# A hybrid attention layer on one core: where the stick-breaking output norm is written, and which engine adds the two halves of an attention output

## Chip, core and metric

The kernel runs on one core of one Trainium2 chip. The metric is device time in microseconds, from the first to the last instruction and what lies around them; lower is better. The five engines each work through their own queue in order: PE (TensorE, matmuls; PEld is its weight load), ACT (ScalarE), DVE (VectorE), POOL (GpSimd) and SP (SyncE, which here issues the DMA transfers).

## What is computed

One layer of a transformer step for 1088 tokens: 1024 of a prompt and 64 of a sample with 128 cached positions. Eight heads use stick-breaking attention, eight use forgetting attention (a causal softmax with a bias), each of 64 channels. Each group of eight heads has an RMS norm of its own over its 512 channels, and then comes one output projection. Cut to what the change touches:

```python
o_sb = sb_prompt(q_sb, k_sb, v_sb)            # 8 heads, each a = exp(...) then a @ v
o_fx = fox_prompt(q_fx, k_fx, v_fx, f_cum)    # 8 heads, softmax(...) @ v
o = concatenate([rmsnorm(o_sb, g_sb_out), rmsnorm(o_fx, g_fox_out)], axis=-1)
x = x + (1.0 + ada[2]) * (o @ w_o)
# rmsnorm(x, g) = x * rsqrt(mean(x * x) + 1e-6) * g ; a SwiGLU FFN follows
```

## The kernel before

Products of fp32 numbers are made of two rounded halves each (hi and lo), so one product is three matmuls (L429, L430, L431, 24 for a block of 128 channels with its 1024 inputs). Channels lie on the 128 partitions, tokens along the free axis, in three chunks CH of 384, 384 and 320 tokens.

The 16 heads go in eight pairs (loop L992 to L1006): pairs 0 to 3 are stick-breaking, 4 to 7 forgetting. For each pair the code writes, in this order, the load of the next pair's weights, attention(pr), project_pair(pr + 1), values, setup of the next pair's head 0, low_finish(), setup of head 1, and low_job(pr + 1). A scheduler puts each engine's instructions in an order of its own, so products of the next pair's projection run among the attention of this one; but tiles of one tag share a fixed number of buffers, and PSUM has eight banks: "acc" 1 (projection products), "z" 3 (scores), "t" 2 (transposes), "u" 1, "av" 1.

attention(pr) (L669) goes through two heads, each with nine query tiles in the order 6, 7, 0, 1, 4, 5, 2, 3, 8, wide ones in two parts, so 13 parts to a head. Of a forgetting head, each part is scored in ps_z (L693, L696, mask L700), its maximum taken by DVE (L721; negated in nm, L727 or L730), its exp made by ACT into a_t (L733, tag "zs", six buffers), normalised by POOL (L739), transposed by PE into pt_a (L748), rounded by ACT (L443) with the rest by DVE (L754), and multiplied by the values into ps_av (L757). In a stick-breaking head sigmoids and a scan kp (L712) stand in place of the exp. av_out (L655) adds the two halves of ps_av into ot: in pairs 0 to 3 by an ACT copy (L662) and a POOL sum (L663), in pairs 4 to 7 by one DVE reduce (L665). L667 stores ot to oT_d in HBM. A hook of attention is a function that is called behind a step; below pair 7 a step is a head.

The norm of the stick-breaking outputs. low_job(5) writes o_stats: the outputs of pairs 0 to 3 are loaded back (L141), added, squared (L829) and summed into sqacc (L831, L834; tag "low", one buffer), beside attention(5). low_finish then writes token_cols (L198) once per chunk: matmuls L204 of 128 tokens by a column of ones into a "u" bank, a scale and epsilon (L212, L215), and rstd_cols (Sqrt on ACT, L191, and five DVE operations, L192 to L196) into cols_sb[c]. low_job(6) then writes sb_norm(0) and sb_norm(2), so ahead of attention(6): spread (L223) broadcasts the columns into a bank bc_o ("u" for chunk 0, "acc" for chunk 2), sum_o (L836, four times) loads an output's two parts o and o_lo (o_lo of tag "zs", as a_t) and adds them on POOL (L840), and DVE scales them (L897). sb_norm(1) and the splits for the output projection are in sb_ready, ahead of attention(7).

Of the kernel before, what the change touches and what calls it, by code (L numbers as in the profile page):

```python
# [8 lines left out]
F32 = mybir.dt.float32  # L9
# [3 lines left out]
ALU = mybir.AluOpType  # L13
# [3 lines left out]
P = 128  # L17
# [4 lines left out]
T = NP + NS  # L22
# [6 lines left out]
CH = ((0, 384), (384, 384), (768, 320))  # L29
# [32 lines left out]
HK = (1, 2)  # L62
# [3 lines left out]
SBT = ('u', 'acc', 'acc')  # L66
SBE = (0, 2)
# [22 lines left out]
def f32(ap):  # L90
    return ap.bitcast(F32)
# [3 lines left out]
def tile_hybrid_trunk(  # L95
# [11 lines left out]
    act, dve, pool, pe, sync = nc.scalar, nc.vector, nc.gpsimd, nc.tensor, nc.sync  # L107
# [13 lines left out]
    for kind, base in (("sb", -1), ("fox", 0)):  # L121
# [4 lines left out]
            out=mf, in_=mf, pattern=[[-1, P]], compare_op=ALU.is_ge,  # L126
# [59 lines left out]
    def bank(tag, name):  # L186
        return ps.tile([P, 512], F32, tag=tag, bufs=bank_bufs[tag], name=name)
# [10 lines left out]
    def token_cols(sqs, toks, count, col, tag="u"):  # L198

        pc = bank(tag, "pc")  # L200
        n = len(toks)
        for j, (a, w) in enumerate(toks):
            for i, sq in enumerate(sqs):
                pe.matmul(  # L204
                    out=pc[:w, j:j + 1], lhsT=sq[:, a:a + w], rhs=ones[:, 0:1],
                    start=(i == 0), stop=(i == len(sqs) - 1))
        v, tmp = col[:, 0, 0:n], col[:, 1, 0:n]
        last = toks[-1][1]
        full = n if last == P else n - 1
        if full < n:  # L210
            dve.memset(v[:, full:n], 1.0)
            dve.tensor_scalar(  # L212
                out=v[:last, full:n], in0=pc[:last, full:n], scalar1=1.0 / count, scalar2=EPS,
                op0=ALU.mult, op1=ALU.add)
        dve.tensor_scalar(  # L215
            out=v[:, 0:full], in0=pc[:, 0:full], scalar1=1.0 / count, scalar2=EPS, op0=ALU.mult, op1=ALU.add)
        rstd_cols(v, tmp)

    def spread(out_bank, col, toks):

        o = 0
        for j, (_, w) in enumerate(toks):
            pe.matmul(  # L223
                out=out_bank[:, o:o + w], lhsT=col[:w, 0, j:j + 1].to_broadcast([w, P]),
                rhs=ident[:w, :w], start=True, stop=True)
            o += w

    def chunk_toks(c, base=0):
        c0, n = CH[c]
        return tuple((base + a, min(P, n - a)) for a in range(0, n, P))  # L230
# [8 lines left out]
    ap1 = attA.enter_context(tc.tile_pool(name="attA1", bufs=1))  # L239
# [29 lines left out]
    def t_low(name, dt=F32):  # L269
        return ap1.tile([P, T], dt, tag="low", name=name)  # L270
# [17 lines left out]
    def load_x(c):  # L288
# [15 lines left out]
    pv = bank("u", "pv")  # L304
# [8 lines left out]
        out=cs4[:, :, 2:4], in0=csil.rearrange("p s k -> p k s"), in1=f32(cs4[:, :, 0:2]), op=ALU.subtract)  # L313
# [341 lines left out]
    def av_out(ps_av, pr, hb, qt):  # L655

        c0, n, t0 = (0, P, qt * P) if qt < 8 else (P - NS, NS, NP)
        ot = ap2.tile([P, 2, P], F32, tag="ot", bufs=OB, name="ot")
        pv = ps_av.rearrange("p (i q) -> p i q", i=2)[:, :, c0:c0 + n]
        piece = ot[:, 0, :n]  # L660
        if pr < 4:
            act.copy(out=ot[:, :, :n], in_=pv)  # L662
            pool.tensor_tensor(out=piece, in0=piece, in1=ot[:, 1, :n], op=ALU.add)  # L663
        else:
            dve.tensor_reduce(  # L665
                out=piece, in_=pv.rearrange("p i q -> p q i"), axis=mybir.AxisListType.X, op=ALU.add)
        sync.dma_start(out=oT_d[pr, hb].rearrange("i d t -> (i d) t")[:, t0:t0 + n], in_=piece)  # L667

    def attention(pr, heads, hooks):  # L669
# [148 lines left out]
    def o_stats(c, acc):  # L818

        t0, n = CH[c]  # L820
        for i in range(0, 4, 2):
            both = [
                t_.rearrange("p a b -> p (a b)")[:, 0:2 * n].rearrange("p (k t) -> p k t", k=2)
                for t_ in (t_lowraw(), f32(ap1.tile([P, 4, 256], F32R, tag="ada_l", name="sq_l")))]
            for k in range(2):
                load_o([t_[:, k] for t_ in both], i + k, t0, n)
            sq = both[0]
            pool.tensor_tensor(out=sq, in0=sq, in1=both[1], op=ALU.add)
            act.activation(sq, sq, AF.Square)  # L829
            if i == 0:  # L830
                pool.tensor_tensor(out=acc, in0=sq[:, 0], in1=sq[:, 1], op=ALU.add)  # L831
            else:
                for k in range(2):
                    pool.tensor_tensor(out=acc, in0=acc, in1=sq[:, k], op=ALU.add)  # L834
# [42 lines left out]
    vv0 = values(0, raws[2])  # L877
    heads = [setup(0, hb, raws[0], raws[1], vv0) for hb in range(2)]
    x1 = [[None] * 3 for _ in range(KT)]
    cols_sb = [ap1.tile([P, 2, 3], F32, name=f"cols_sb{c}") for c in range(3)]  # L880

    sb_o = [None] * 3

    def sb_norm(c, tag):

        t0, n = CH[c]
        bc = bank(tag, "bc_o")
        spread(bc, cols_sb[c], chunk_toks(c))
        if c < 2:
            o = [t_[:, a:a + n] for t_ in (t_low("o32"), t_lowraw().rearrange("p a b -> p (a b)")) for a in (0, n)]  # L890
        else:
            t_ = ap1.tile([P, 4, 256], F32, tag="ada_l", name="o32").rearrange("p a b -> p (a b)")
            o = [t_[:, a:a + n] for a in (0, n, 2 * n)] + [ap1.tile([P, n], F32, tag="small", name="o32_3")]
        for k in range(4):
            sum_o(o[k], k, t0, n, pool)
        for k in range(4):
            dve.scalar_tensor_tensor(  # L897
                out=o[k], in0=o[k], scalar=go[:, k:k + 1], in1=bc[:, :n], op0=ALU.mult, op1=ALU.mult)
        sb_o[c] = o
# [7 lines left out]
    def low_job(pr):  # L907

        for job in JOBS[pr]:
            ada_job(job)  # L910
        if pr == 6:
            for c in SBE:
                sb_norm(c, SBT[c])
        if pr != 5:
            return lambda: None
        acc = t_low("sqacc")
        for c, (t0, n) in enumerate(CH):
            o_stats(c, acc[:, t0:t0 + n])

        def finish():  # L920
            for c, (t0, n) in enumerate(CH):
                token_cols([acc[:, t0:t0 + n]], chunk_toks(c), 512, cols_sb[c])
        return finish


    fxh = [[None] * 3 for _ in range(4)]
# [62 lines left out]
        sb_split(1)  # L989

    low_finish = low_job(0)
    for pr in range(8):  # L992
        if pr < 7:
            wqk = load_qk(pr + 1)
        if pr == 7:
            sb_ready()
        attention(pr, heads, {HK[0]: fox_first, HK[1]: fox_second} if pr == 7 else {})
        if pr < 7:
            raws = project_pair(pr + 1, *wqk)
            vv1 = values(pr + 1, raws[2])  # L1000
            heads = [setup(pr + 1, 0, raws[0], raws[1], vv1)]
            low_finish()
            if pr == FG:
                forget_gates()
            heads.append(setup(pr + 1, 1, raws[0], raws[1], vv1))
            low_finish = low_job(pr + 1)  # L1006
# [627 lines left out]
```

## Time and profile before

| | |
|---|---|
| device time, median of 3 runs | 1635.71 us (1634.99 to 1638.09) |
| the profiled execution's own time | 1636.31 us |
| its span, first to last instruction | 1634.5 us |
| busy in the span | PE 94%, DVE 65%, ACT 49%, POOL 47% |
| mean granted clock of PE, of full speed | 0.973 |

Times in the rows are microseconds from the span's start. A row of a timeline gives start, length, engine, line and operation, output and inputs by the program's names, shapes and count, and in brackets the engine's idle time before it with what ended that. A row of stretches gives the stretch and its length, then the busy time of each engine with its count of instructions, PE's granted clock, the share of the DMA engines and GB/s. ACT, DVE and POOL busy times are those of their own instructions; matmul ends are modelled, so neighbouring matmuls overlap in the rows.

### The profile page before, as it was taken

The page shows a single profiled execution, that of the slowest core. Times are in us where ns is not written, and L with a number is a line of the kernel's source. Part 1 is how long each engine was busy: PE and PEld are TensorE (multiplying, and loading weights), DVE is VectorE, ACT ScalarE, POOL GpSimd, SP SyncE. Part 2 cuts the span into 40 slices and gives each one's busy share as a digit, 9 for nine tenths or more (in the row PEclk, how much of TensorE's full clock was granted, in tenths as well). Part 3 has the DMA queues.
Part 4 walks back from the last instruction along what each step waited for, and adds up shares of the span by engine and source line. Part 5 has one row for each costly group of instructions (what it writes and reads, how often), then busy time and mean ns, then how long its engine had stood idle before and what let it go on. Part 6 is the DMA issues. An engine that isn't in the chain of part 4 may idle for free.

```text
span 1634.5 us, 26657 instructions
## 1 busy us (share of the span) xinstructions
PE 1541.7 (94%) x9558; PEld 1445.6 (88%) x9558; DVE 1061.0 (65%) x2061; ACT 804.2 (49%) x1684; POOL 768.4 (47%) x681
## 2 busy tenths in 40 slices
PE   8899998999899986998999999999999999999998
PEld 4698887978788875888999999999999999999997
DVE  5656666578448464667785676657656666666665
ACT  5466656678255553554454454534433333333335
POOL 1557767675668785494343444442222222222222
PEclk9999999999899996999999999999999999999998
DMA  9533332421535463273325554442221222222211
GB/s 305 177 110 93 109 100 85 113 79 29 129 96 141 118 164 90 62 229 95 90 65 155 149 150 146 150 130 77 84 80 51 78 66 64 78 78 78 65 39 78
DMA packets 223204, 174.68 MB, mean 107 GB/s; under 512 B 15488, under 2 KB 213536, under 8 KB 223072
## 3 DMA queue, kind: packets, MB, share of 16 engines
q1 hardware_dynamic: 223072, 172.97, 36.7%
q8 instruction: 76, 1.25, 0.3%
q14 instruction: 56, 0.46, 0.1%
HBM read 138.63 MB, written 27.08 MB: 101 GB/s over the span
## 4 chain that ended last, share of the span: by engine, by line
PE 74%; DVE 8%; POOL 5%; DMA 4%; ACT 4%; issue 3%; SPq 2%; POOLq 0%; ACTq 0%; DVEq 0%
PE gu L1357 19%; PE acc_d L1183 5%; PE acc_d L1185 5%; PE acc_d L1184 5%; PE acc L429 5%; PE acc L430 4%; PE acc L431 4%; PE gu L430 3%; PE gu L431 3%; PE gu L429 3%; PE pt_a L748 3%; PE ps_av L757 2%; PE ps_z L693 2%; PE acc_o L429 1%; PE acc_o L430 1%
## 5 line engine op out<-in xcount | busy, mean ns | idle before, releaser
L1170 ACT CAST whi<-wraw 128x512 fp32r<-128x512 f32 (+1 forms) x209 | 157.0, 776 | 183.7 <-PE acc_d L1185 146.2
L1171 DVE TENSOR_TENSOR wlo<-wraw,whi 128x512 fp32r<-128x512 f32 (+1 forms) x178 | 162.6, 929 | 84.7 <-ACT whi L1170 81.4
L429 PE MATMUL acc<-h,whi 128*128 128x384 f32 (+1 forms) x576 | 200.9, 349 | 3.7 <-ACT qraw L486 1.4
L1206 DVE SCALAR_TENSOR_TENSOR x<-acc_d,ada,x 128x256 f32<-128x256 f32 (+1 forms) x352 | 159.0, 494 | 66.6 <-PE acc_d L1185 65.8
L431 PE MATMUL acc<-h,whi 128*128 128x384 f32 (+1 forms) x576 | 194.6, 338 | 3.5 <-DVE h L406 3.5
L430 PE MATMUL acc<-h,wlo 128*128 128x384 f32 (+1 forms) x576 | 194.5, 338 | 0.0
L1357 PE MATMUL gu<-bT,whi 128*128 128x384 f32 x704 | 187.3, 336 | 0.9 <-ACT u L1371 0.9
L1183 PE MATMUL acc_d<-d,whi 128*128 128x384 f32 (+1 forms) x528 | 175.3, 332 | 3.0 <-DVE h L1286 2.1
L1185 PE MATMUL acc_d<-d,whi 128*128 128x384 f32 (+1 forms) x528 | 173.3, 328 | 0.6 <-DVE d L1519 0.6
L1184 PE MATMUL acc_d<-d,wlo 128*128 128x384 f32 (+1 forms) x528 | 172.8, 327 | 0.0
L754 DVE TENSOR_TENSOR aT<-pt_a,aT 128x384 fp32r<-128x384 f32 (+3 forms) x208 | 111.1, 537 | 60.9 <-ACT aT L443 59.8
L443 ACT CAST aT<-pt_a 128x384 fp32r<-128x384 f32 (+3 forms) x208 | 98.9, 480 | 89.4 <-PE pt_a L748 71.9
L1325 POOL TENSOR_TENSOR s<-wraw 128x512 f32<-128x512 f32 x22 | 28.5, 1296 | 227.9 <-DMA wraw<-in_w_gate 126.8
L1171 POOL TENSOR_TENSOR wlo<-wraw,whi 128x1024 fp32r<-128x1024 f32 x31 | 76.7, 2475 | 125.3 <-ACT whi L1170 120.5
L1357 PEld LDWEIGHTS gu<-bT,whi 128*128 128x128 f32 x704 | 128.1, 188 | 1.7 <-ACT u L1371 1.5
L716 POOL TENSOR_TENSOR a_t<-a_t,kp 128x383 f32<-128x383 f32 (+6 forms) x104 | 94.4, 910 | 62.6 <-DVE kp L712 47.7
L429 PEld LDWEIGHTS acc<-h,whi 128*128 128x128 f32 x576 | 112.6, 195 | 8.6 <-ACT qraw L486 2.5
L748 PE MATMUL pt_a<-ident,a_t 128*128 128x128 f32 x608 | 104.0, 282 | 16.7 <-POOL a_t L739 10.1
L1357 PE MATMUL gu<-bT,wlo 128*128 128x384 f32 x352 | 118.1, 335 | 0.0
L757 PE MATMUL ps_av<-aT,vv 128*128 128x256 f32 x608 | 106.3, 297 | 11.0 <-DVE aT L754 4.2
L431 PEld LDWEIGHTS acc<-h,whi 128*128 128x128 f32 x576 | 111.8, 194 | 4.8 <-DVE h L406 4.1
L430 PEld LDWEIGHTS acc<-h,wlo 128*128 128x128 f32 x576 | 112.5, 195 | 0.6
(359 smaller groups left out, 4252.1 us busy)
## 6 DMA issues: line engine op xcount, KB each, us to landing
wraw<-in_w_gate SPq DMA_DIRECT2D x44, 512.0 KB, 4.1
wraw<-in_w_up SPq DMA_DIRECT2D x44, 512.0 KB, 3.8
wraw<-in_w_down SPq DMA_DIRECT2D x44, 512.0 KB, 3.5
lowraw<-in_w_ada SPq DMA_DIRECT2D x32, 512.0 KB, 3.8
wraw<-in_w_in SPq DMA_DIRECT2D x24, 512.0 KB, 6.0
wa<-in_w_ada SPq DMA_DIRECT2D x16, 512.0 KB, 6.3
oT_d<-ot SPq DMA_DIRECT2D x128, 64.0 KB, 2.9
wraw<-in_w_o SPq DMA_DIRECT2D x11, 512.0 KB, 3.8
```

The source lines that it names most:

```text
L429: pe.matmul(out=acc, lhsT=wh[:, kt, :], rhs=rh[kt], start=st, stop=False)
L430: pe.matmul(out=acc, lhsT=wl[:, kt, :], rhs=rh[kt], start=False, stop=False)
L431: pe.matmul(out=acc, lhsT=wh[:, kt, :], rhs=rl[kt], start=False, stop=sp_)
L748: pe.transpose(out=pt[:, j * P:(j + 1) * P], in_=at[a][:, j * P:(j + 1) * P], identity=ident)
L757: pe.matmul(out=ps_av, lhsT=vv[:, v0 + j, :], rhs=aT[:, j, :], start=(ci == 0 and j == 0), stop=(ci == len(parts) - 1 and j == nb - 1))
L1170: act.copy(out=hi, in_=src)
L1171: lo_eng.tensor_tensor(out=lo, in0=src, in1=f32(hi), op=ALU.subtract)
L1183: pe.matmul(out=a_, lhsT=wh[:, m, :], rhs=dh, start=first, stop=False)
L1184: pe.matmul(out=a_, lhsT=wl[:, m, :], rhs=dh, start=False, stop=False)
L1185: pe.matmul(out=a_, lhsT=wh[:, m, :], rhs=dl, start=False, stop=not first)
L1206: dve.scalar_tensor_tensor(out=xc[:, a:b], in0=acc[:, a:b], scalar=ada[:, 5, m, s:s + 1], in1=xc[:, a:b], op0=ALU.mult, op1=ALU.add)
L1357: pe.matmul(out=acc, lhsT=w_[:, k, :], rhs=bh[BAND[i], k, r_], start=(i in (0, 1, 3) and k == 0 and j == 0), stop=(k == 3 and j == 2), ski ...
```

## The change

In av_out all pairs add the two halves by the DVE reduce. The three tiles cols_sb[c] become one of nine columns, filled by one call of token_cols over nine tiles of 128 tokens (the last of 64). That call, sb_norm(0) and sb_norm(2) are put into a function sb_early, which is a hook behind step 0 of attention(6), that is behind the first head of the seventh pair. low_finish has nothing left to do. o_stats stays in low_job(5), and sb_norm(1) in sb_ready.

```diff
--- before.py
+++ after.py
@@ -658,12 +658,8 @@
         ot = ap2.tile([P, 2, P], F32, tag="ot", bufs=OB, name="ot")
         pv = ps_av.rearrange("p (i q) -> p i q", i=2)[:, :, c0:c0 + n]
         piece = ot[:, 0, :n]
-        if pr < 4:
-            act.copy(out=ot[:, :, :n], in_=pv)
-            pool.tensor_tensor(out=piece, in0=piece, in1=ot[:, 1, :n], op=ALU.add)
-        else:
-            dve.tensor_reduce(
-                out=piece, in_=pv.rearrange("p i q -> p q i"), axis=mybir.AxisListType.X, op=ALU.add)
+        dve.tensor_reduce(
+            out=piece, in_=pv.rearrange("p i q -> p q i"), axis=mybir.AxisListType.X, op=ALU.add)
         sync.dma_start(out=oT_d[pr, hb].rearrange("i d t -> (i d) t")[:, t0:t0 + n], in_=piece)
 
     def attention(pr, heads, hooks):
@@ -877,15 +873,22 @@
     vv0 = values(0, raws[2])
     heads = [setup(0, hb, raws[0], raws[1], vv0) for hb in range(2)]
     x1 = [[None] * 3 for _ in range(KT)]
-    cols_sb = [ap1.tile([P, 2, 3], F32, name=f"cols_sb{c}") for c in range(3)]
 
     sb_o = [None] * 3
+    sqacc = []
+    cols_sb = ap1.tile([P, 2, 9], F32, name="cols_sb")
+
+    def sb_early():
+
+        token_cols([sqacc[0]], [(a, min(P, T - a)) for a in range(0, T, P)], 512, cols_sb)
+        for c in SBE:
+            sb_norm(c, SBT[c])
 
     def sb_norm(c, tag):
 
         t0, n = CH[c]
         bc = bank(tag, "bc_o")
-        spread(bc, cols_sb[c], chunk_toks(c))
+        spread(bc, cols_sb[:, :, 3 * c:3 * c + 3], chunk_toks(c))
         if c < 2:
             o = [t_[:, a:a + n] for t_ in (t_low("o32"), t_lowraw().rearrange("p a b -> p (a b)")) for a in (0, n)]
         else:
@@ -908,19 +911,13 @@
 
         for job in JOBS[pr]:
             ada_job(job)
-        if pr == 6:
-            for c in SBE:
-                sb_norm(c, SBT[c])
         if pr != 5:
             return lambda: None
-        acc = t_low("sqacc")
+        sqacc.append(t_low("sqacc"))
         for c, (t0, n) in enumerate(CH):
-            o_stats(c, acc[:, t0:t0 + n])
-
-        def finish():
-            for c, (t0, n) in enumerate(CH):
-                token_cols([acc[:, t0:t0 + n]], chunk_toks(c), 512, cols_sb[c])
-        return finish
+            o_stats(c, sqacc[0][:, t0:t0 + n])
+
+        return lambda: None
 
 
     fxh = [[None] * 3 for _ in range(4)]
@@ -989,12 +986,13 @@
         sb_split(1)
 
     low_finish = low_job(0)
+    hooks = {6: {0: sb_early}, 7: {HK[0]: fox_first, HK[1]: fox_second}}
     for pr in range(8):
         if pr < 7:
             wqk = load_qk(pr + 1)
         if pr == 7:
             sb_ready()
-        attention(pr, heads, {HK[0]: fox_first, HK[1]: fox_second} if pr == 7 else {})
+        attention(pr, heads, hooks.get(pr, {}))
         if pr < 7:
             raws = project_pair(pr + 1, *wqk)
             vv1 = values(pr + 1, raws[2])
```

## Rows read from the trace of the kernel before

**Rows 1.** The page's first part: busy us (share of span), x instructions

```profile
PE 1541.7 (94%) x9558; PEld 1445.6 (88%) x9558; DVE 1061.0 (65%) x2061; ACT 804.2 (49%) x1684; POOL 768.4 (47%) x681
```

**Rows 2.** Stretches: length, busy us of PE, PEld, DVE, ACT, POOL; PEclk, DMA share

```profile
120.00:440.00 320.00, 295.15 (x1933) 263.42 (x1933) 209.50 (x338) 200.42 (x470) 218.53 (x238) 0.96 0.33 90
606.50:619.40 12.90, 7.05 (x38) 5.03 (x37) 6.01 (x15) 3.06 (x8) 10.41 (x11) 0.84 0.72 185
619.40:645.70 26.30, 13.18 (x50) 10.94 (x51) 11.69 (x42) 9.46 (x25) 15.58 (x20) 0.50 0.38 101
645.70:679.30 33.60, 33.51 (x220) 31.80 (x220) 19.07 (x57) 15.69 (x44) 15.96 (x17) 0.99 0.19 50
```

**Rows 3.** ACT timeline: start, length, line, operation, idle before and its releaser

```profile
605.13 0.43 ACT L733 ACTIVATE a_t<-ps_z,nm 128x192 f32<-128x192 f32 x1
...
621.53 1.28 ACT L191 ACT_TABLE_LOAD   x1
622.82 0.20 ACT L191 ACTIVATE cols_sb<-cols_sb 128x3 f32<-128x3 f32 x1
...
633.88 0.58 ACT L733 ACTIVATE a_t<-ps_z,nm 128x384 f32<-128x384 f32 x1 [2.30 <-POOL o L840]
...
670.38 0.58 ACT L733 ACTIVATE a_t<-ps_z,nm 128x384 f32<-128x384 f32 x1
...
694.59 0.41 ACT L733 ACTIVATE a_t<-ps_z,nm 128x192 f32<-128x192 f32 x1
```

**Rows 4.** POOL timeline from 598 to 644

```profile
598.18 2.37 POOL L178 TENSOR_TENSOR wlo<-wraw,whi 128x1024 fp32r<-128x1024 f32 x1
...
626.62 1.79 POOL L834 TENSOR_TENSOR sqacc<-sqacc,lowraw 128x320 f32<-128x320 f32 x2 [0.85 <-ACT lowraw L829]
...
629.54 0.86 POOL L840 TENSOR_TENSOR o<-o,o_lo 128x320 f32<-128x320 f32 x1 [1.13 <-DMA o_lo<-oT_d]
...
642.76 0.87 POOL L840 TENSOR_TENSOR o<-o,o_lo 128x320 f32<-128x320 f32 x1
```

**Rows 5.** PE timeline: last product of projection(6), column sums, projection(7)

```profile
593.78 0.31 PE L431 MATMUL acc<-h,whi 128*128 128x320 f32 x1
...
628.47 1.32 PE L204 MATMUL pc<-ones,sqacc 128*128 128x1 f32 x6 [4.19 <-DVE cols_sb L195]
...
645.75 0.49 PE L429 MATMUL acc<-h,whi 128*128 128x384 f32 x1
...
646.25 0.34 PE L431 MATMUL acc<-h,whi 128*128 128x384 f32 x1
646.42 0.34 PE L429 MATMUL acc<-h,whi 128*128 128x384 f32 x1
```

**Rows 6.** DVE timeline: pair 6, head 0, first nm and last output

```profile
608.02 0.20 DVE L727 TENSOR_SCALAR nm<-mx 128x1 f32<-128x1 f32 x1
...
678.97 0.29 DVE L665 TENSOR_REDUCE ot<-ps_av 128x64 f32<-128x128 f32 x1 [1.48 <-PE ps_av L757]
```

**Rows 7.** Stretches as in rows 2, of line L429 alone

```profile
645.70:679.30 33.60, 13.85 (x40) 7.41 (x40) 0.99 0.19 50
```

**Rows 8.** SP timeline, issue of two loads of o_lo

```profile
694.87 1.14 SPq L141 DMA_DIRECT2D o_lo<-oT_d  x2
```

**Rows 9.** Groups by line and form: busy us, mean ns, idle before

```profile
L757 PE MATMUL ps_av<-aT,vv 128*128 128x256 f32 x608 | 106.3, 297 | 11.0 <-DVE aT L754 4.2 <-DVE ot L665 3.5 <-ACT ot L662 3.2
...
L662 ACT COPY ot<-ps_av 128x256 f32<-128x256 f32 x64 | 24.6, 384 | 18.3 <-PE ps_av L757 11.3 <-issue 3.6 <-POOL wlo L178 1.5
...
L663 POOL TENSOR_TENSOR ot<-ot 128x128 f32<-128x128 f32 x64 | 32.4, 509 | 11.1 <-issue 5.7 <-ACT ot L662 5.3
...
L665 DVE TENSOR_REDUCE ot<-ps_av 128x128 f32<-128x256 f32 x64 | 26.7, 418 | 22.5 <-PE ps_av L757 21.4 <-DMA o_lo<-oT_d 0.7
```

**Rows 10.** Waits of PE in 120 to 440: us, times, longest

```profile
PE pt_a L748 <- DVE aT L754: 4.5, 8, 1.0
...
PE ps_z L693 <- DVE kp L712: 2.6, 5, 0.9
```

## Prediction

> **What bounds the kernel now.** I read four views, from coarse to fine. The page's first part says that PE is busy for 94% of the span [rows 1], so outside its idle stretches only work taken off PE, or a wait of PE taken away, counts. The table by stretches then shows where PE is not busy around the lines of the diff. During the stick-breaking pairs (120 to 440) PE runs 295.2 of 320.0 us, and POOL is the next engine (218.5), ahead of DVE (209.5) and ACT (200.4). From 606.5 to 645.7 it runs 7.05 + 13.18 = 20.2 of 39.2 us, at a granted clock of 0.84 and then 0.50, the lower of its two levels (1.2 GHz). Right behind, from 645.7 to 679.3, it runs 33.5 of 33.6 us at 0.99 [rows 2]. So 19 us of PE are empty in one place, and that place is where the norm of the diff sits.
>
> The third view is ScalarE's timeline there. The last exp of pair 5 starts at 605.13, the first of pair 6 at 633.88, and it is released by POOL's sum `o` of L840, not by its own scores [rows 3]: these are the eight sums of o and o_lo (L840, 629.54 to 643.63) that sb_norm(0) and sb_norm(2) write ahead of attention(6) [rows 4]. Their o_lo tiles and the exps' a_t tiles are of one tag, "zs", with six buffers. Buffers of a tag go round in the order in which the code asks for them, so pair 6's head 0 gets none until o_lo tiles have been read, and these wait for the column sums, whose last input is POOL's L834 (626.62 + 1.79 = 628.41): PE's last six passes L204 start at 628.47 [rows 4, 5]. The fourth view, PE's own, gives the other end. Projection(7)'s first product in bank "acc" starts at 645.75 [rows 5], because sb_norm(2)'s bc_o holds that one bank until the last sum (642.76 + 0.87) and its scaling are done [rows 4]. From there PE is full; the end of the kernel moves with the work that is left for PE at that point.
>
> **Change, part by part.** *(a) The hook.* Token_cols and the two sb_norm move from ahead of attention(6) to behind its head 0. In the written order head 0's a_t tiles now come before the o_lo tiles. Its first maximum is ready (nm, 608.02 + 0.20) [rows 6], so its exps start at about 608 instead of 633.9. A head whose exps are not held spends 670.38 to 694.59 + 0.41, so 24.6 us, on its exps with products of a projection in between [rows 3]; head 0 then has its last exp at about 608 + 24.6 = 633 and its last output at 637 to 640. That is a bit slower than it could be with an empty PE, because POOL must share head 0's normalisations with the end of o_stats and setup(6, 1) until 628.4 [rows 4].
>
> What this is worth: in 645.7 to 679.3 PE did all of head 0's remaining work, up to its last reduce at 678.97 [rows 6]. The projection had 40 + 40 + 39 = 119 products there (the row shows the 40 of L429; L430 and L431 had 40 and 39 in the same stretch) [rows 7], at one per 0.17 us (646.25 to 646.42) [rows 5], so 20.2 us. The other 33.5 − 20.2 = 13.3 us are head 0, less some 0.8 for head 1's first scores: **12.5 us** of PE work go out of a full stretch into an empty one.
>
> What takes the place of the stall: behind head 0 come the same 18 passes, eight sums and eight scalings, and acc still goes to bc_o before it goes to projection(7) (written later). The o_lo loads now wait for a_t buffers, from about 632 on. From the first L840 to projection(7) took 645.75 − 629.54 = 16.2 us before [rows 4, 5], part of it DMA waits between sums; the o tiles' buffers are free much earlier now, so I take 632 + 14.7 = 646.7: **1 us later** (bounds 642 and 652, that is −3.7 to +6.3).
>
> SP: the 32 loads of the eight sums move behind pair 6's first output stores, 0.57 us each (1.14 for two, 694.87) [rows 8], so some 18 us of SP's order; they may hold up stores of head 1, for which nobody waits, and the cast weights of projection(7) are in place already (L178 ends 600.55) [rows 4]. Cost 0. That the o_lo at 694.87 was issued right at the end of the exp of 694.59 [rows 3, 8] is the same hand-over of "zs" buffers at the next pair.
>
> The added wait: PE issues in order, and the passes L204 wait for sqacc until 628.41. Where they stand in PE's order ahead of head 0's transposes, these queue behind them, and who waits for that is head 0's exps (through its scores) and its stores. Bounds 0 and about 4.2 us (the idle time ahead of 628.47) [rows 5]; the stretch is empty, so 0 of it reaches the end as long as projection(7) is bound by bc_o; I take 0.
>
> *(b) One chain of columns.* PE passes stay 18. Two of three Sqrt and twelve of the twenty small DVE operations go; what is left works on nine columns and lies beside head 0 or 1, so 0. The Sqrt now stands among exps and needs its two table loads as before, 1.28 us each, with the Sqrt starting 0.01 us behind the load (621.53 + 1.28, 622.82) [rows 3]: 2.6 us of ACT beside idle PE. The Trainium skill ("ScalarE: Activation LUTs", What ACT_TABLE_LOAD costs) prices a switch at 1283 ns and a drain of about 1380 ns more; the row has no room for a drain, and by the page's price the two would be 5.3 us of ACT, in the same cover.
>
> *(c) av_out in pairs 0 to 3.* Of 72 outputs 64 are full and eight are smaller. By form, ACT copies of 384 ns (64 are 24.6 us, with the rest under 27.6) and POOL sums of 509 ns (32.4, under 36.6) go; DVE reduces of 418 ns (26.7, under 30.1) come [rows 9]. In 120 to 440 DVE then has some 209.5 + 29 = 238 of 320 us (75%), POOL 184, ACT 174 [rows 2]. No row shows a reduce in these pairs. Nearest are PE's waits there: 3.2 us for ot by L662, which goes, and 4.5 + 2.6 us behind DVE (aT of L754, kp of L712), which a fuller DVE would lengthen [rows 10]. Bounds −3.2 (all of the first gone) and +7.1 (the second doubled); over pairs 4 to 7, L665 let PE wait 3.5 us where L662 in pairs 0 to 3 let it wait 3.2, as the row of L757 has it [rows 9], so I take 0.
>
> **Sum.** 1636.3 (the profiled execution's own time; the median of the runs is 0.6 lower) − 12.5 + 1 + 0 + 0 = 1624.8, say **1625.0 us**. Its own range is 1617 to 1638 by the bounds above (−3.7 − 3.2, +6.3 + 7.1).
>
> **Rivals.** *A, more than head 0 fills the stall.* If acc were not handed out in written order but to whoever is ready, projection(7) would start before 645.7 too: its weights have been ready since 600.55, acc has been empty since 593.9 (last product L431 at 593.78) [rows 4, 5]. All 19 idle us go, and the clock of 0.50 in 619.4 to 645.7 costs 13.2 / 2 = 6.6 us less [rows 2]: 1636.3 − 25 = 1611. Against it: the same readiness stood there before and PE still sat idle. Chance 0.10.
> *B, the chain only shifts.* The norm behind head 0 takes as long as before, counted from head 0's last exp: 633 + 8 for the loads of the first buffers and 16.2 for the sums gives projection(7) at about 657, 11.5 late, and 11.5 of the 12.5 are eaten: 1635.3. For it: the sums were spaced by DMA waits. Against: six buffers come free one by one before the last exp. Chance 0.14.
> *C, slower: head 0 without cover.* Head 0 took from 633.88 to 679.26, 45.4 us, when it shared its engines [rows 3, 6]. If POOL (o_stats, setup) and PE's wait in L204 make it as long from 608, it ends at 653.4; the sums from there take 14.1 us (629.54 to 643.63) and the start 2 more, so projection(7) starts at 669.5, 23.7 late. 1636.3 − 12.5 + 23.7 = 1647.5. It decides against the change from a projection(7) that starts after 645.75 + 12.5 = 658.2. Against it: those 45.4 us also held five chunks of products, 20.2 us [rows 7]. Chance 0.12.
> *D, DVE becomes the bound in pairs 0 to 3.* The reduce stands in DVE's order between the scans (L712) and subtractions (L754) that PE waits for. With 29 us more, a third of it showing (+10), the whole is 1635. Against: DVE at 75% still has a quarter free, and POOL, the fuller engine, is relieved. Chance 0.08. The Trainium skill ("VectorE: DVE Perf Modes", Rules for kernel authors) calls tensor_reduce on a hot path the slowest DVE operation, to be restructured; the row of 0.418 us against 0.384 + 0.509 for the pair that it replaces makes it the cheaper one here, and by the rule D would be the likeliest.
>
> **How the numbers follow.** Forecast 0.56, A 0.10, B 0.14, C 0.12, D 0.08. The predicted time is the forecast's, 1625.0. The range 1611 to 1640 takes in A, B, D and the forecast's own bounds and leaves out C and A's far side. Within 0.2% (3.3 us, about what a measurement of this kernel can tell from no change) lie B and D for the most part and a twentieth of the forecast: faster 0.65, same 0.18, slower 0.17.
>
> **What would show it.** Right: the first exp of pair 6 near 608 instead of 633.9; L204's last passes and L223 among or behind head 0's matmuls; the first product of projection(7) at 642 to 652; PE busy for about 33 of the 39 us up to it; head 1's end and pair 7's first scores some 11 us earlier; 29 us more of DVE in 120 to 440 with waits of PE for ot and aT of the same size. Wrong: a first product before 640 (A), at 655 to 660 (B), after 660 (C), or pair 4 starting several us later than before (D).

## Result

The changed kernel takes 1622.84 us (median of 5 runs, 1621.5 to 1624.91) against 1636.57 us before (median of 5): a ratio of 0.9917 with a 95% interval of 0.9903 to 0.9930, so 13.7 us less. The forecast was 1625.0 in 1611 to 1640. The number came out; two of the terms that it was added up from did not, as the parts below show. The profiled execution has a span of 1621.0 us.

The line numbers of the changed kernel lie a few lower: L739 is now L735, L733 is L729, L757 is L753, L748 is L744, L840 is L836, L667 is L663, L665 is L661. First the page's busy times and the same four stretches as in rows 1 and 2:

```profile
PE 1537.0 (95%) x9558; PEld 1440.3 (89%) x9558; DVE 1076.9 (66%) x2121; ACT 782.2 (48%) x1608; POOL 734.3 (45%) x609
```
```profile
120.00:440.00 320.00, 302.14 (x2018) 271.52 (x2017) 239.67 (x431) 190.62 (x416) 194.61 (x171) 0.98 0.34 93
606.50:619.40 12.90, 11.78 (x89) 9.90 (x87) 11.76 (x39) 9.68 (x31) 11.83 (x17) 1.00 0.30 81
619.40:645.70 26.30, 13.76 (x72) 10.42 (x70) 13.34 (x38) 9.50 (x21) 13.34 (x18) 0.78 0.50 135
645.70:679.30 33.60, 32.64 (x204) 31.36 (x205) 17.77 (x52) 16.13 (x41) 18.50 (x19) 0.92 0.29 78
```

In 120 to 440 DVE has 30 us more, as reckoned, and PE got 85 more matmuls done than before: the kernel is ahead long before the hook. The stretch in which the stall stood is fuller at first (11.8 of 12.9 us) and then as empty as it was (13.8 of 26.3). ScalarE's timeline, as rows 3:

```profile
596.57 0.43 ACT L729 ACTIVATE a_t<-ps_z,nm 128x192 f32<-128x192 f32 x1
...
601.42 0.59 ACT L729 ACTIVATE a_t<-ps_z,nm 128x384 f32<-128x384 f32 x1
...
628.23 1.28 ACT L191 ACT_TABLE_LOAD   x1
629.52 0.21 ACT L191 ACTIVATE cols_sb<-cols_sb 128x9 f32<-128x9 f32 x1
...
636.04 1.28 ACT L729 ACT_TABLE_LOAD   x1 [4.12 <-DMA o_lo<-oT_d]
637.34 0.58 ACT L729 ACTIVATE a_t<-ps_z,nm 128x384 f32<-128x384 f32 x1
```

Pair 5's last exp is at 596.57 and pair 6's first at 601.42: the 29 us without an exp are gone from that place. A gap of 16.7 us stands behind head 0 now (its last exp is at 620.67, head 1's first at 637.34). PE's timeline, as rows 5:

```profile
616.68 1.48 PE L204 MATMUL pc<-ones,sqacc 128*128 128x1 f32 x12
...
626.72 0.71 PE L204 MATMUL pc<-ones,sqacc 128*128 128x1 f32 x6
...
630.87 0.77 PE L753 MATMUL ps_av<-aT,vv 128*128 128x256 f32 x2 [1.39 <-DVE cols_sb L195]
631.43 2.95 PE L223 MATMUL bc_o<-ident,cols_sb 128*128 128x128 f32 x12
...
650.44 0.52 PE L429 MATMUL acc<-h,whi 128*128 128x384 f32 x1
```

The column sums run among head 0's matmuls, head 0's last product ends at 631.64, and projection(7) starts at 650.44. That is 4.7 us later than before by the clock of the span, though everything ahead of it is 7 us early.

The table gives five events in the traces of the kernels that are compared below (us from the span's start): the first product of projection(4), the end of pair 5's last product L757, the first product of projection(7), the first of the output projection (acc_o), and the first of the FFN (gu).

| kernel | projection(4) | pair 5 ends | projection(7) | acc_o | gu |
|---|---|---|---|---|---|
| before | 378.0 | 619.3 | 645.7 | 720.2 | 861.5 |
| the change | 368.6 | 612.2 | 650.4 | 712.0 | 847.8 |
| e1, sums only | 368.5 | 609.2 | 635.1 | 711.9 | 852.8 |
| e2, hook only | 379.7 | 623.9 | 661.9 | 724.4 | 858.0 |
| e3, all but the hook | 369.4 | 610.9 | 637.5 | 713.0 | 854.5 |
| e4, the change, bank u | 368.7 | 618.8 | 584.9 | 684.6 | 821.4 |
| e12, e4 without the hook | 368.2 | 618.1 | 585.6 | 694.3 | 831.7 |

### The profile page after: what moved, and what is told of

Read it like the earlier page. It is cut to its first block, busy times and chain, and to the rows that moved or that the text cites. A ratio compares the mean times of both kernels' runs of the same rounds, so it can differ in the third digit from the quotient of the medians.

```text
span 1621.0 us, 26463 instructions
## 1 busy us (share of the span) xinstructions
PE 1537.0 (95%) x9558; PEld 1440.3 (89%) x9558; DVE 1076.9 (66%) x2121; ACT 782.2 (48%) x1608; POOL 734.3 (45%) x609
## 4 chain that ended last, share of the span: by engine, by line
PE 65%; DVE 7%; DMA 3%; ACT 3%; POOL 2%; issue 2%; SPq 0%; ACTq 0%; DVEq 0%; POOLq 0%
PE gu L1355 19%; PE acc_d L1181 5%; PE acc_d L1183 5%; PE acc_d L1182 5%; PE gu L430 3%; PE gu L431 3%; PE gu L429 3%; PE acc L429 2%; PE acc L430 2%; PE ps_av L753 2%; PE acc L431 2%; PE pt_a L744 2%; PE acc_o L429 2%; PE acc_o L430 2%; PE acc_o L431 2%
## 5 line engine op out<-in xcount | busy, mean ns | idle before, releaser
L429 PE MATMUL acc<-h,whi 128*128 128x384 f32 (+1 forms) x576 | 199.5, 346 | 4.7 <-ACT vraw L443 2.6
L429 PEld LDWEIGHTS acc<-h,whi 128*128 128x128 f32 x576 | 111.8, 194 | 8.3 <-ACT vraw L443 3.1
L744 PE MATMUL pt_a<-ident,a_t 128*128 128x128 f32 x608 | 102.2, 281 | 17.8 <-POOL a_t L735 8.7
L753 PE MATMUL ps_av<-aT,vv 128*128 128x256 f32 x608 | 106.9, 297 | 11.6 <-DVE ot L661 6.0
```

Source lines behind the costliest of these rows:

```text
L429: pe.matmul(out=acc, lhsT=wh[:, kt, :], rhs=rh[kt], start=st, stop=False)
L744: pe.transpose(out=pt[:, j * P:(j + 1) * P], in_=at[a][:, j * P:(j + 1) * P], identity=ident)
L753: pe.matmul(out=ps_av, lhsT=vv[:, v0 + j, :], rhs=aT[:, j, :], start=(ci == 0 and j == 0), stop=(ci == len(parts) - 1 and j == nb - 1))
```

## Experiments

The kernel before was timed anew beside each group of runs, with medians of 1635.3 to 1637.3 us, so a difference between runs of two groups is uncertain by about 2 us. Events are read from one traced execution of each kernel.

**Which part of the change brings the time?** e1 has only the DVE sums, in the kernel before:

```diff
-        if pr < 4:
-            act.copy(out=ot[:, :, :n], in_=pv)
-            pool.tensor_tensor(out=piece, in0=piece, in1=ot[:, 1, :n], op=ALU.add)
-        else:
-            dve.tensor_reduce(
-                out=piece, in_=pv.rearrange("p i q -> p q i"), axis=mybir.AxisListType.X, op=ALU.add)
+        dve.tensor_reduce(
+            out=piece, in_=pv.rearrange("p i q -> p q i"), axis=mybir.AxisListType.X, op=ALU.add)
```

> Only the two sums of pairs 0 to 3 go to the DVE reduce; three chains of columns and the norm ahead of attention(6), as before. As predicted (the sums are worth 0, the hook 11.5): 1636 us, within 3 of before. Rival, read from the trace after the change, where pair 5's last output product ends at 612.2 instead of 619.3: the sums are worth about 7 us, all of it ahead of pair 6, so 1629 us, with pair 5's end some 7 us earlier and the stall in front of projection(7) as long as before (39 us).

Measured: 1628.24 us against 1636.74, ratio 0.9945 (0.9931 to 0.9958). The sums are worth 8.5 us. e2 is the other half, the changed kernel with the old lines of av_out:

> Only the one chain of columns and the hook behind pair 6's head 0; in pairs 0 to 3 ACT copies and POOL adds the two sums, as before. As predicted: 1625 us, projection(7) from about 647. Rival: projection(7) starts some 11 to 12 us later than before (about 657), which takes back the 12.5 us of head 0: 1635 us. If the other half of the gain after the change (5.5 us in the output projection) belongs to the hook, about 1629 us.

Measured: 1632.01 us, 0.9969 (0.9952 to 0.9985): 4.7 us. The two halves add up to 13.2 of 13.7. The hook alone, for which 1625 was forecast, lies between the marks of the other two expectations, 1629 and 1635. e3 keeps the single chain of columns and the DVE sums, but not the place:

```diff
     def low_job(pr):
+        if pr == 6:
+            for c in SBE:
+                sb_norm(c, SBT[c])
...
-        return lambda: None
+        return chain
...
-    hooks = {6: {0: sb_early}, 7: {HK[0]: fox_first, HK[1]: fox_second}}
+    hooks = {7: {HK[0]: fox_first, HK[1]: fox_second}}
```

> The whole change except the place: one chain of columns, written where the three were (ahead of setup of pair 6's head 1), sb_norm(0) and sb_norm(2) ahead of attention(6); DVE sums everywhere. As predicted (place is worth 11.5): 1636 us. Rival (place is worth nothing, the sums 7): the time of the kernel with the sums alone, about 1629 us, or a few us worse, because chunk 0's and 1's columns now wait for chunk 2's.

Measured: 1630.33 us, 0.9959 (0.9944 to 0.9974). It stands 2.1 us above e1, with intervals that overlap; in its trace PE's wait ahead of the last column sums is 5.03 us where e1's is 3.93. That one chain by itself brings anything is not shown. The place is worth 5.4 us (to e1) to 7.5 us (to e3).

**What holds projection(7)?** e4 changes one word of the changed kernel: bc_o of chunk 2 goes into bank u.

```diff
-SBT = ('u', 'acc', 'acc')
+SBT = ('u', 'acc', 'u')
```

> The whole change, and bc_o of chunk 2 goes into bank u instead of acc (one word). If bank acc, handed out in written order, is what holds projection(7): its first product comes near 613 instead of 650, the stall of about 26 us between 619 and 646 fills with products, and the time falls by 12 to 20 us, to 1603 to 1611. If something else holds it (the scheduler's order, weights, a tile of the projection): 1623, as with the change, or slower by the wait of pair 7's transposes for bank u.

Measured: 1597.02 us, 0.9754 (0.9738 to 0.9770), 25.8 us below the change and 39.7 below before, more than the 12 to 20 us that were expected. PE's timeline and the two stretches of the stall in e4:

```profile
584.89 0.42 PE L429 MATMUL acc<-h,whi 128*128 128x384 f32 x1
```
```profile
606.50:619.40 12.90, 12.87 (x86) 12.27 (x85) 8.57 (x26) 8.91 (x26) 11.78 (x13) 1.00 0.49 139
619.40:645.70 26.30, 24.02 (x160) 22.20 (x158) 18.95 (x50) 14.65 (x34) 18.57 (x20) 0.94 0.49 132
```

Projection(7) follows right behind projection(6), 65 us earlier than with the change, and PE runs 36.9 of the 39.2 us that were half empty. So bank acc had held it, and not weights or an order of the scheduler. e12 asks what the hook is worth when acc is free. It is e3 with the word of e4:

```diff
-SBT = ('u', 'acc', 'acc')
+SBT = ('u', 'acc', 'u')
...
-    hooks = {6: {0: sb_early}, 7: {HK[0]: fox_first, HK[1]: fox_second}}
+    hooks = {7: {HK[0]: fox_first, HK[1]: fox_second}}
```

> Bank u for bc_o of chunk 2, one chain and DVE sums, but the norm where it was before the change, ahead of attention(6). If bank acc alone made the stall in front of projection(7): its first product at 585 to 600, head 0 still held by the o_lo tiles, 1597 to 1603 us, so the hook is worth little once acc is free. If the hook is needed for it: 1615 to 1625.

Measured: 1606.75 us, 0.9827 (0.9804 to 0.9849). Projection(7) starts at 585.6 here too; the word alone lifts the stall, and by itself it is worth 23.6 us (to e3). The expectation that the hook is worth little once acc is free was wrong: it is worth 9.7 us (to e4), nearer to the 12.5 that had been forecast for it than the 4.7 to 7.5 with acc held.

**Why does projection(7) start so late with the change?** The timelines of POOL (the sums) and SP behind the hook, in the changed kernel:

```profile
632.18 0.99 POOL L836 TENSOR_TENSOR o<-o,o_lo 128x384 f32<-128x384 f32 x1 [6.10 <-DMA o<-oT_d]
...
642.22 0.86 POOL L836 TENSOR_TENSOR o<-o,o_lo 128x320 f32<-128x320 f32 x1 [1.69 <-DMA o_lo<-oT_d]
644.86 0.86 POOL L836 TENSOR_TENSOR o<-o,o_lo 128x320 f32<-128x320 f32 x1 [1.78 <-DMA o_lo<-oT_d]
647.46 0.86 POOL L836 TENSOR_TENSOR o<-o,o_lo 128x320 f32<-128x320 f32 x1
```
```profile
631.69 1.00 SPq L663 DMA_DIRECT2D oT_d<-ot  x2
632.74 0.45 SPq L141 DMA_DIRECT2D lowraw<-oT_d  x1
633.25 0.59 SPq L141 DMA_DIRECT2D o_lo<-oT_d  x1
633.88 1.23 SPq L141 DMA_DIRECT2D lowraw<-oT_d  x2
635.15 2.51 SPq L141 DMA_DIRECT2D o_lo<-oT_d  x4
637.71 1.24 SPq L141 DMA_DIRECT2D o<-oT_d  x2
639.04 1.18 SPq L141 DMA_DIRECT2D o_lo<-oT_d  x2
640.27 1.23 SPq L141 DMA_DIRECT2D o<-oT_d  x2
641.60 2.46 SPq L141 DMA_DIRECT2D o_lo<-oT_d  x4
```

Eighteen of the hook's 32 loads leave SP without a break from 632.74 to 644.06, at 0.6 us each, four for a sum; they stand in SP's order behind the stores of head 0's last outputs, and the last four sums follow each other at 2.6 us. But that is the lesser part. From pair 5's end to projection(7) the change takes 38.3 us and e1, which has the norm in its old place, 26.0: 12.3 us more. The first sum comes 20.0 us behind pair 5's end (e1 10.0), and from its start to the end of the last it is 16.1 us (e1 13.9), so 10.0 of the 12.3 us lie ahead of the sums. The last sums into sqacc on POOL and the first load of an o tile of chunk 0, in the change and then in e1, there with its first sum of o:

```profile
624.26 1.81 POOL L830 TENSOR_TENSOR sqacc<-sqacc,lowraw 128x320 f32<-128x320 f32 x2
628.74 1.09 SPq L141 DMA_DIRECT2D o<-oT_d  x2
```
```profile
616.17 1.79 POOL L830 TENSOR_TENSOR sqacc<-sqacc,lowraw 128x320 f32<-128x320 f32 x2 [0.85 <-ACT lowraw L825]
619.14 0.86 POOL L836 TENSOR_TENSOR o<-o,o_lo 128x320 f32<-128x320 f32 x1 [1.17 <-DMA o_lo<-oT_d]
619.36 2.36 SPq L141 DMA_DIRECT2D o<-oT_d  x4
```

sqacc is ready 13.9 us behind pair 5's end, in e1 8.8; in between POOL now runs eight normalisations of head 0 (6.1 us), in e1 none. The column sums wait for sqacc. Two o tiles of chunk 0 take sqacc's own buffer (tag "low", one buffer), so their loads wait for the last column sums: these end at 627.43, and the load at 628.74 goes behind one load and one store more (in e1 they end at 619.33 and the load goes at 619.36). In the change chunk 0's sums come first, at 632.18 behind that load; in e1 chunk 2's, which do not need this buffer. This is read from the traces; no run changed the buffer or POOL's order.

Two experiments were to take issues off SP. e6 loads each tile of the hook by one transfer (one is true there alone), with another layout of oT_d; the first edit is the store, L663, the second load_o:

```diff
-        sync.dma_start(out=oT_d[pr, hb].rearrange("i d t -> (i d) t")[:, t0:t0 + n], in_=piece)
+        sync.dma_start(out=oT_d[pr, :, hb, :, t0:t0 + n], in_=piece)
...
         for i, t_ in enumerate(tiles):
+            if one:
+                sync.dma_start(out=t_, in_=oT_d[k, i].rearrange("e d t -> (e d) t")[:, t0:t0 + n])
+                continue
             for e in range(2):
-                sync.dma_start(out=t_[e * HD:(e + 1) * HD], in_=oT_d[k, e, i, :, t0:t0 + n])
+                sync.dma_start(out=t_[e * HD:(e + 1) * HD], in_=oT_d[k, i, e, :, t0:t0 + n])
```

> The whole change; the eight sums of the hook load each tile by one transfer of 128 partitions instead of two of 64 (oT_d is laid out with the two halves outside the two heads for it), so 16 issues on SP instead of 32. All other loads stay in two. Theory SP: behind the hook SP issues from 620 to 644 without a break at 0.6 us each, and the sums L836 follow each other at 2.5 us, four issues; with half the issues projection(7) starts 6 to 9 us earlier (642 to 645 instead of 650), and the time falls by about as much, to some 1615. Rival, buffers: the sums wait for a_t buffers of tag zs and for the latency of a transfer; then projection(7) starts within 2 us of 650 and the time stays at 1623.

Measured: 1639.54 us, 1.0017 (1.0003 to 1.0030), 0.2% above before. The sums themselves did what SP's theory says, 10.4 us from the first to the end of the last where the change has 16.1:

```profile
641.46 1.00 POOL L839 TENSOR_TENSOR o<-o,o_lo 128x384 f32<-128x384 f32 x1 [3.59 <-DMA o_lo<-oT_d]
643.12 1.01 POOL L839 TENSOR_TENSOR o<-o,o_lo 128x384 f32<-128x384 f32 x1 [0.66 <-DMA o_lo<-oT_d]
646.52 1.96 POOL L839 TENSOR_TENSOR lowraw<-lowraw,o_lo 128x384 f32<-128x384 f32 x2 [2.40 <-DMA o_lo<-oT_d]
648.43 3.44 POOL L839 TENSOR_TENSOR o<-o,o_lo 128x320 f32<-128x320 f32 x4
```

But the kernel was 9.1 us behind the change before the hook was reached (pair 5 ends at 621.3), and projection(7) started at 653.5. Behind pair 5's end that is 32.2 us instead of 38.3, while the first sum still comes 20.2 us behind it: half the issues shorten the sums and not what lies ahead of them. The other layout has a price of its own: a store of an output took SP 498 ns (median of 144) where the change's takes 326. So e6 is no clean test of the total. e9 is e4 with the same layout and every load in one transfer:

```diff
-SBT = ('u', 'acc', 'acc')
+SBT = ('u', 'acc', 'u')
...
         for i, t_ in enumerate(tiles):
-            for e in range(2):
-                sync.dma_start(out=t_[e * HD:(e + 1) * HD], in_=oT_d[k, e, i, :, t0:t0 + n])
+            sync.dma_start(out=t_, in_=oT_d[k, i].rearrange("e d t -> (e d) t")[:, t0:t0 + n])
```

> Bank u for bc_o of chunk 2 (1597 us measured) and one transfer for every load of an output tile, those of o_stats and of the forgetting norm too. With acc free the sums no longer hold projection(7), only pair 6's head 1; if SP's issues still matter there and in pair 7: 1590 to 1595. If SP is hidden now: 1597 within 2.

Measured: 1638.11 us, 1.0010 (0.9998 to 1.0021), 41 us above e4. It loses 16.3 us up to pair 5's end (635.1 against 618.8) and 21.3 in the output projection. The longer stores may be part of that; the cause was not tried and stays open. e10 leaves layout and transfers as they are and lets ACT issue the loads of the tiles o; qs_ is (act, sync) in the hook and (sync, sync) elsewhere:

```diff
-                sync.dma_start(out=t_[e * HD:(e + 1) * HD], in_=oT_d[k, e, i, :, t0:t0 + n])
+                qs_[i].dma_start(out=t_[e * HD:(e + 1) * HD], in_=oT_d[k, e, i, :, t0:t0 + n])
```

> The whole change; of the hook's 32 loads the 16 of the tiles o are issued by ACT, the 16 of o_lo by SP as before; layout, sizes and number of transfers stay. Theory SP (the sums L836 wait for SP to issue four loads of 0.6 us for each): the spacing of the sums falls from 2.5 to some 1.3 us, projection(7) starts at 642 to 645 instead of 650, and the time falls by 5 to 8 us, to 1615 to 1618. Rival, buffers and latency: projection(7) within 2 us of 650, 1623 us; if ACT's issues hold up head 1's exps, up to 1628.

Measured: 1619.11 us, 0.9892 (0.9868 to 0.9915); the interval overlaps that of the change. The traced execution was the slowest of five (1623.65). In its trace SP has 11 loads left behind the last stores:

```profile
634.73 1.56 SPq L663 DMA_DIRECT2D oT_d<-ot  x2
636.35 6.84 SPq L141 DMA_DIRECT2D o_lo<-oT_d  x11
```

Head 0's last product ended 4.0 us later than with the change (635.6), and projection(7) started at 649.6, so 14.0 us behind it instead of 18.8. Seven issues fewer on SP behind the stores are 4.3 us at 0.61, and the distance shrank by 4.8. But by the sign that had been set, projection(7) within 2 us of 650, this is the rival's outcome. Behind pair 5's end the first sum comes at 19.2 us (20.0 with the change) and projection(7) at 35.4 (38.3), so half of the loads off SP take back 2.8 of the 12.3 us. ACT's first o load for chunk 0 goes at 629.48, 0.08 us behind the last column sum: there the buffer holds it, and no order of SP. SP's issues are a part of the price, then, and not the whole, and the gain in the total cannot be told from none.

**Why are the sums worth 8.5 us?** In pairs 0 to 3, e7 (the first diff, to the changed kernel) frees POOL and e8 (the second) frees ACT:

```diff
+        if pr < 4:
+            act.copy(out=ot[:, :, :n], in_=pv)
+            dve.tensor_tensor(out=piece, in0=piece, in1=ot[:, 1, :n], op=ALU.add)
```
```diff
+        if pr < 4:
+            dve.tensor_copy(out=ot[:, :, :n], in_=pv)
+            pool.tensor_tensor(out=piece, in0=piece, in1=ot[:, 1, :n], op=ALU.add)
```

> The whole change, but in pairs 0 to 3 ACT copies ps_av as before and DVE, not POOL, adds the two halves. ACT is loaded as before the change, POOL is free of the sums. Theory POOL (the sums' gain is POOL's relief: the split ada_l of the side jobs gets done earlier, its buffer lowraw is reloaded earlier, PE waits less for ada_h): within 2 us of the change, 1621 to 1625. Theory ACT (the relief of ACT's queue counts): like the kernel with the hook alone, 1631 to 1633.

> The mirror image: in pairs 0 to 3 DVE copies ps_av and POOL adds the two halves as before. ACT is free, POOL loaded as before the change, DVE has about as much more as with the reduces. Theory POOL: like the kernel with the hook alone, 1631 to 1633. Theory ACT: within 2 us of the change, 1621 to 1625. If neither single relief is enough, both lie between.

Measured: e7 1634.84 us, 0.9990 (0.9979 to 1.0001); e8 1619.16 us, 0.9889 (0.9866 to 0.9911). Freeing ACT is enough. e7 came out above both of its theories, and it is no clean counterpart, as PE's waits in its 120 to 440 say (us, times, longest), and, of ACT's copy L662, who waited for it:

```profile
PE pt_a L748 <- DVE aT L754: 17.4, 18, 5.6
PE ps_z L693 <- DVE kp L712: 3.5, 5, 1.6
```
```profile
  DVE ot L663: 20.6, 15
```

DVE's sum waits for ACT's copy (20.6 us in 15 times), and behind it in DVE's order wait the subtractions aT that PE needs: 17.4 us where before has 4.5 [rows 10]. So e13 took POOL's sums away and put nothing in their place:

```diff
         if pr < 4:
             act.copy(out=ot[:, :, :n], in_=pv)
-            pool.tensor_tensor(out=piece, in0=piece, in1=ot[:, 1, :n], op=ALU.add)
```

> One chain and the hook, and in pairs 0 to 3 ACT copies ps_av as before, but POOL's 72 sums of the two halves are left out, so the outputs of the stick-breaking heads lack their second half. POOL is free of the sums, ACT is loaded as before the change, and no engine takes over. Theory ACT (the copies on ACT are what costs the 8 to 13 us): like the kernel with the hook alone, 1630 to 1634. Theory POOL (the sums on POOL cost): 1620 to 1624.

Measured: 1619.10 us (1614.67 to 1626.9), 0.9897 (0.9875 to 0.9920). Freeing POOL is enough too, and the theory that ACT alone counts falls. What both free is a chain that runs over both engines. Beside pairs 0 to 4 the code writes side jobs (ada_job); each loads lowraw twice, ACT rounds it (L779), POOL subtracts (L780), PE multiplies the two parts into bank u, and lowraw can be loaded anew only when POOL has read it. Behind the last job of pair 2, bank u goes to the transposes of pair 3's rows and values and to the forget gates (pt_lt), and bank acc goes to the gates' products and then to projection(4), in the order in which they are written. Timelines of that chain's end ahead of projection(4): POOL's and PE's before, then POOL's and PE's in e1:

```profile
319.64 2.38 POOL L780 TENSOR_TENSOR ada_l<-lowraw,ada_h 128x1024 fp32r<-128x1024 f32 x1
328.03 2.40 POOL L780 TENSOR_TENSOR ada_l<-lowraw,ada_h 128x1024 fp32r<-128x1024 f32 x1
```
```profile
357.69 0.30 PE L551 MATMUL pt_v<-ident,vraw 128*64 128x128 f32 x1
370.70 0.34 PE L608 MATMUL pt_lt<-ident,fg 8*128 8x8 f32 x3
...
377.95 0.45 PE L429 MATMUL acc<-h,whi 128*128 128x384 f32 x1
```
```profile
316.71 3.57 POOL L776 TENSOR_TENSOR ada_l<-lowraw,ada_h 128x1024 fp32r<-128x1024 f32 x1
```
```profile
349.43 0.27 PE L551 MATMUL pt_v<-ident,vraw 128*64 128x128 f32 x1
358.70 0.35 PE L608 MATMUL pt_lt<-ident,fg 8*128 8x8 f32 x3
...
368.50 0.45 PE L429 MATMUL acc<-h,whi 128*128 128x384 f32 x1
```

The last ada_l ahead of projection(4) starts 11.3 us earlier in e1, projection(4) 9.5 us, the FFN 8.7. Over six kernels the last transposes of the side jobs ahead of projection(4) (pt_ada, ends 335.3, 325.4, 337.0, 339.5, 326.3 and 330.5 in before, e1, e2, e7, e8 and e13) and the first product of projection(4) (378.0, 368.5, 379.7, 383.4, 369.5 and 371.3) lie 40.8 to 43.9 us apart, also in e7 and e13, whose traced executions were the slowest of theirs (1639.76 and 1626.9): the chain moves as a whole. The chain shows in PE's waits too. Of PE's waits from 120 to 440 the largest row before is the one for ada_h; e1 has almost none of it left (us, times, longest; before, then e1):

```profile
PE pa L784 <- ACT ada_h L779: 5.5, 2, 3.4
```
```profile
PE pa L780 <- ACT ada_h L775: 0.4, 1, 0.4
```

That it is this chain which carries the 8.5 us is read from these traces; no run shortened the side jobs alone.

**Both findings together:** bank u, and e8's copy by DVE with POOL's sum.

```diff
-SBT = ('u', 'acc', 'acc')
+SBT = ('u', 'acc', 'u')
...
+        if pr < 4:
+            dve.tensor_copy(out=ot[:, :, :n], in_=pv)
+            pool.tensor_tensor(out=piece, in0=piece, in1=ot[:, 1, :n], op=ALU.add)
```

> Bank u for bc_o of chunk 2, and in pairs 0 to 3 DVE copies ps_av and POOL adds. If the two gains lie in different places and add (1597.0 with bank u; 3.7 us less with DVE's copy than with its reduce): 1593 us. If the 3.7 us were the scheduler's luck in one order: 1595 to 1600.

Measured: 1594.12 us (1592.12 to 1597.71), 0.9747 (0.9723 to 0.9770), the fastest of all; its interval overlaps that of e4, so the gain of the copy over the reduce is not shown on top of it.

## Why the number was right and the working was not

*The sums (part c): wrong.* They were taken at 0 within −3.2 and +7.1, and are worth −8.5, outside the bounds. The busy times were right (some 30 us more of DVE, with 3.3 us of waits for ot and 3.8 for aT after). The step that failed is the choice of the waits that made the bounds: only those for the outputs that the change touches and for DVE were taken. Left out was the largest of PE's waits in the stretch, 5.5 us for ACT's ada_h of the side jobs, though ACT and POOL, which the change relieves, work through these jobs; e1 leaves 0.4 of it. PE idles 24.9 us from 120 to 440 before and 17.9 with the change, so this wait is most of the difference. And a bank came back: the side jobs' chain ended 10 us earlier ahead of projection(4), and with it the handing on of u and acc to that projection. That acc is given out in written order was known for projection(7), and was not asked of the other projections. Rival D is refuted by e1.

*The hook's gain (part a): right in place and size.* From projection(7)'s start to acc_o the kernel takes 74.5 us before and 61.6 with the change (12.9 less), 76.8 in e1 against those 61.6 (15.2 less); 12.5 were forecast. Head 0's exps start right behind pair 5's.

*Projection(7)'s start: wrong, and it ate that gain.* It was put 1 us later, at most 6.3. By the clock of the span 650.4 lies within the stated 642 to 652, but only because the sums had brought everything ahead of it forward; the hook alone (e2) has it at 661.9, 16.2 us later than before. Against e1 the change has it 15.3 us later, 12.3 of them behind pair 5's end. From head 0's last exp to projection(7) the forecast had 633 to 646.7, so 13.7 us; the change takes 29.8 (620.67 to 650.44). Three steps failed. PE's passes L204 were taken to wait for sqacc until 628.41, 9.1 us behind pair 5's end, at a cost of 0; with head 0's normalisations ahead of it on POOL, sqacc is ready at 13.9 us. The buffers of the o tiles were taken to be free much earlier; two of chunk 0's tiles take sqacc's buffer and had to wait for these same passes, so that the sums start 20.0 us behind pair 5's end. And 18 us of SP's issues were counted rightly and costed at nothing, with the reason that no one waits for the stores of head 1. The ones who wait are the sums; before, eight o_lo loads had left SP between 606.77 and 616.32, among other work, while the column sums were still to come. The sums' own part is 2.3 us (16.1 against 13.9). That is rival B, whose chain runs from head 0's last exp: it gave 24.2 us to projection(7), of which 16.2 behind the first sum, where 29.8 and 18.3 were measured, and the hook alone, at 1632.0, is nearer to B's 1635.3 than to the forecast. What B did not name is why the first sum comes late.

*What made up for it: not foreseen.* From acc_o to the FFN the kernel takes 141.3 us before and 135.8 after, for the same 130.4 and 130.8 us of busy PE; in e1 it is 140.9, in e2 133.6, so it goes with the hook. The wait of 3.74 us below stands in e1 (3.77) and e3 (3.90) too, and not in e2. PE's timelines of the same place in pair 7, before and after:

```profile
778.48 0.69 PE L429 MATMUL acc_o<-h,whi 128*128 128x384 f32 x1 [3.74 <-ACT a_t L733]
```
```profile
763.80 1.03 PE L753 MATMUL ps_av<-aT,vv 128*128 128x256 f32 x4 [1.21 <-DVE ot L661]
```

With the hook, pair 6 is out of the way before the output projection starts: its last product ends at 685.1, acc_o starts at 712.0 (before 717.9 and 720.2). ACT has 146 instructions left in that part instead of 153, DVE 262 instead of 270, and the wait of 3.74 us is gone. This is read from the traces of before, after, e1, e2 and e3, and was not tried by itself.

*The sum:* forecast −12.5 + 1 + 0 = −11.5. Measured −8.5 for the sums and −4.7 to −5.4 for the hook with its one chain. Stage by stage the hook (the change against e1, and e2 against before) is +3.0 and +4.6 up to pair 5's end, +12.3 and +11.6 from there to projection(7), −15.2 and −12.0 from there to acc_o, −5.1 and −7.7 in the output projection. Of the first pair of numbers the beginning of head 0, which now runs beside the end of pair 5, may be a part; in e2 1.7 us of it are there at projection(1) already (112.6 against 110.9), ahead of every line that the hook changes, and what they are stays open. That the forecast number was met is luck: errors of −8.5, +11 and −5 us nearly cancel.

*Rival A* was wrong for the change (projection(7) does wait for acc) and right about the size of what lies there: it put 25 us on filling the stall with the norm in its old place, and e12, which lets acc go there, is 23.6 us below e3; with the hook (e4 against the change) it is 25.8.

*The two rules weighed.* The slow tensor_reduce of the Trainium skill ("VectorE: DVE Perf Modes", Rules for kernel authors) made no bound here: one of 0.42 us took the place of 0.38 on ACT and 0.51 on POOL, and the kernel gained. The drain behind a table load of the Trainium skill ("ScalarE: Activation LUTs", What ACT_TABLE_LOAD costs) does not show after the change either: the load at 628.23 takes 1.28 us and the Sqrt starts at 629.52.

## What to carry to other kernels

Ask of each bank and buffer that goes round in written order who gets it next and who stands behind that one: here one word, the bank of a small broadcast, was worth 25.8 us, nearly twice the whole change. Work that is moved behind other work shares engines, buffers and queues with it: here the moved chain waited for POOL, for a buffer that its own first step still read, and for SP's issues. So follow each link again from its new place before a cost of 0 is written down, and look at every wait of the engine that bounds the kernel, not only at those that name the tiles of the change. And when a forecast is met, take the change apart all the same: its halves were worth 8.5 and 4.7 us where 0 and 11.5 had been reckoned.

## What the runs showed of the hardware

In the changed kernel a transfer of 64 partitions took SP 0.59 to 0.63 us to issue when issues stood back to back (1.18 to 1.24 for two, 2.46 to 2.51 for four), and in e6 a store whose side in HBM has one dimension more (the two halves apart) took 0.50 us where the plain one took 0.33. Eleven loads in a row took 6.84 us in e10, so 0.62 each. In the kernel before, PE's longer stalls went with a lower granted clock: the stretch from 430 to 440, with the wait of 3.40 us ahead of 431.82, had a mean of 0.66, those with waits of 2.1 to 2.4 us (270 to 280, 410 to 420, 530 to 540) 0.83 to 0.87, and the one with a wait of 1.28 us (380 to 390) 1.00.
